# A two-layer hybrid encoder: residual rows, post-norm gains and memory operands issued at single steps of the output projection, and three memory steps ahead of layer two

## The chip, the cores and the metric

The kernel runs on one core of a Trainium2 chip. The metric is the device time of one execution in microseconds (us). Engines are named as in the profile: PE (TensorE, matmul), PEld (its weight loads), DVE (VectorE), ACT (ScalarE), POOL (GpSimd) and SP (SyncE). POOL and SP do hardly more here than issue DMAs; queue q0 is POOL's, queue q1 is SP's.

## What is computed

Two layers, each with the same parts. Sequence 512, width 2048, 256 memory tokens, all in float32:

```python
for l in range(2):
    h = rmsnorm(x, pre_norm_g[l])
    z = h @ w_in[l]                       # splits: latents, conv parts, memory query, gate
    a_out = mla_attention(...)            # from the latents
    c_out = short_gated_conv(...)
    mem_n = rmsnorm(mem, mem_norm_g[l])
    m_out = memory_attention(q_mem, mem_n, w_mk[l], w_mv[l])   # mk = mem_n @ w_mk, mv = mem_n @ w_mv
    y = concat([a_out, c_out, m_out]) * silu(gate)
    o = y @ w_o[l]                        # 2048 x 2048: the output projection
    x = x + rmsnorm(o, post_norm_g[l])    # post-norm and residual
```

## The kernel before

**Number format.** Each float32 operand is split into a high part (`wh`, a rounding cast on ACT, L179) and a low part (`wl`, the difference, on DVE, L180). One product is three matmuls: high by high, high by low, low by high (L252 to L254). A weight must have been loaded (`wr`), cast and subtracted before its matmuls can start; the first of a step needs `wh`, the second `wl`.

**The products.** A projection multiplies blocks of two by two in seven products, P1 to P7, instead of eight. The output projection runs in two pairs of output columns, `g0` and `g1`, 2 x 512 columns each. Each is a list of passes: P2, P1, P5, P6, then P3 and P7 alternating, then P4. A pass has four steps, c = 0 to 3, one for each 256 rows of a quarter of the weights; a step is twelve matmuls. P3/P7 has eight steps. The P2 passes of both pairs run earlier, inside the attention. What is left of a pair, `g0[1:]` or `g1[1:]`, is P1 (steps 1 to 4), P5 (5 to 8), P6 (9 to 12), P3/P7 (13 to 20), P4 (21 to 24).

**Weights.** Sums of weight blocks are formed in two ways. P1 loads a block into a tile T; P5 adds a second block on DVE (L170); P6 and P4 add a third and a fourth by an *accumulating load* (`more`, L135 with `accum_op`), which POOL issues into the same `wr` tile as soon as the last reader of its older contents is done. P7 adds a block to P3's on DVE (L170). All other loads are plain ones that SP issues (512 KB each). There are eight `wr` tiles; four of them hold T all through a pair, so P3 and P7 have four. There are three `wh` and three `wl` tiles. In layer two's second pair the split of P4's weights goes into slabs of its own, `T4h` and `T4l`.

**Around it.** `fetch(t)` loads row block t of the residual (`xr`, 1 MB) on POOL; `gains(g)` loads the two post-norm gain blocks of a pair (`g2`, 256 KB each) on POOL. When a row block has its four column blocks, `residual` sums the squares, adds the row block to the residual (L1162), writes it to `xs`, and in layer one normalises it (L543, L549) for layer two. `mem_reload` reads the transposed, split memory (`mH`, `mL`, two of each, 1 MB apiece) back from DRAM on POOL. Layer two begins with sixteen memory steps (`mk`, `mv`), between which the normalised rows are transposed (`hps`, L562), sixteen groups of four; step t waits for row block t.

**Order.** PE, SP and POOL execute in the order in which the program is written, with weights prepared two steps ahead. The order on DVE and ACT is set by a scheduler from dependences and its own estimates, so it can change where the text of those engines does not.

Of the kernel before, what the change touches and what calls it, by code (L numbers as in the profile page):

```python
# [6 lines left out]
F32R = mybir.dt.float32r  # L7
# [9 lines left out]
NT = S // P  # L17
# [61 lines left out]
class Program:  # L79
# [19 lines left out]
    def add(self, fn, units=(), room=0.0, ahead=None):  # L99

        self.steps.append((list(units), fn, room, self.ahead if ahead is None else ahead))
# [106 lines left out]
def encoder(tc, x, mem, positions, pre_norm_g, w_in, q_norm_g, w_uq, kv_norm_g, w_ukv, conv_w,  # L208
# [3 lines left out]
    nc = tc.nc  # L212
    depth = w_in.shape[0]
# [15 lines left out]
    add = pr.add  # L229

    G = {}
    n_id = [0]

    def nm(s):
        n_id[0] += 1
        return f"{s}_{n_id[0]}"
# [4 lines left out]
    def slab(name, dt=F32):  # L241
        return slabs.tile([P, D], dt, tag="slab", name=nm(name))
# [310 lines left out]
    def transpose_rows(l, t, src, quarters=range(4), on=None):  # L553

        if quarters[0] == 0:
            G[f"hT{t}"] = slab("hT").rearrange("p (k c) -> p k c", c=P)
        hT = G[f"hT{t}"]
        g = G[f"g1_{l}"].rearrange("p (k o) -> p k o", o=1)
        for q in quarters:
            ps = bank("hps")  # L560
            for j in range(4):
                nc.tensor.transpose(ps[:, j * P:(j + 1) * P], src[:, (4 * q + j) * P:(4 * q + j + 1) * P], G["ident"])  # L562
            if (on or (nc.vector if t < 2 else nc.scalar)) is nc.vector:
                nc.vector.tensor_tensor(hT[:, 4 * q:4 * q + 4, :], ps.rearrange("p (j c) -> p j c", j=4),
                                        g[:, 4 * q:4 * q + 4, :].broadcast_to([P, 4, P]), op=ALU.mult)
            else:
                for j in range(4):
                    nc.scalar.activation(hT[:, 4 * q + j, :], ps[:, j * P:(j + 1) * P], AF.Copy,
                                         scale=g[:, 4 * q + j, :])

    def left_half(tt, halves=(0, 1)):
        hT = G[f"hT{tt}"]
        for h in halves:
            G["left"].split(("A11", "A12")[h], tt, hT[:, 8 * h:8 * h + 8, :])
# [11 lines left out]
    def first_factor(t):  # L586
        G[f"hs{t}"] = slab("hs")
        G[f"r{t}"] = row_factor(G[f"x{t}"], G[f"hs{t}"])

    def first_rows(t, halves=(0, 1)):  # L590
        for h in halves:
            c = slice(h * 1024, (h + 1) * 1024)
            nc.vector.tensor_scalar_mul(G[f"hs{t}"][:, c], G[f"x{t}"][:, c], G[f"r{t}"])
# [78 lines left out]
            for i in range(2):  # L672
                nc.gpsimd.dma_start(G["mTd"][2 * (q // 4) + i], G["mT"][-1][i].bitcast(F32))

    def mem_reload(h):
        two = slab("mH", F32R), slab("mL", F32R)
        for i in range(2):
            nc.gpsimd.dma_start(two[i], G["mTd"][2 * h + i])
        G.setdefault("mT", []).append(two)

    def mem_kt(kt, sl=slice(None)):
        return tuple(t.rearrange("p (k c) -> p k c", c=256)[:, kt % 8, sl] for t in G["mT"][kt // 8])
# [506 lines left out]
    def put(*passes):  # L1189
        for steps in passes:  # L1190
            for s in steps:
                add(*s)
# [26 lines left out]
    for l in range(depth):  # L1219
        G["left"] = L = Left(True)  # L1220
        C, gs, owns = projection(l)

        def use(L=L):
            G["left"] = L
            G["ys"] = {}
        turn = [lambda l=l, t=t: transpose_rows(l, t, G[f"hs{t}"]) for t in range(NT)]
        if l == 0:
            add(use)
            def turn_half(t, h, on=None):
                return lambda: transpose_rows(0, t, G[f"hs{t}"], (2 * h, 2 * h + 1), on)  # L1230
            add(turn_half(0, 0))
            add(lambda: first_rows(1, (0,)))
            add(pr.begin_prep(1))
            add(lambda: left_half(0, (0,)))
            add(pr.begin_prep(2))
            add(turn_half(1, 0, nc.scalar))
            add(lambda: first_rows(1, (1,)))
            add(lambda: left_half(1, (0,)))
            add(pr.begin_prep(3))
            add(lambda: first_factor(2))  # L1240
            add(turn_half(0, 1))
        else:
            ms = mem_steps(l)
            put(ms[:1])
            add(use)
            for n in range(16):
                t, q = n // 4, n % 4
                if q == 0:
                    add(lambda t=t: pr.until(lambda: f"hs{t}" in G))
                add(lambda t=t, q=q: transpose_rows(l, t, G[f"hs{t}"], (q,)))  # L1250
                if t < 2 and q % 2:
                    add(lambda t=t, q=q: left_half(t, (q // 2,)))
                if t >= 2 and q == 3:
                    add(lambda t=t: right_half(t - 2))
                put(ms[n + 1:n + 2])
        (a, b), (a1, b1) = gs[0][:2], gs[1][:2]
        add(owns[0])
        if l == 0:
            put(a[:1])
            add(first.close)  # L1260
            add(turn_half(1, 1))
            add(lambda: left_half(0, (1,)))
            add(lambda: left_half(1, (1,)))
            add(lambda: first_rows(2))
            add(lambda: first_factor(3))
            add(lambda: first_rows(3))
            put(a[1:], b[:1])
            add(turn[2])
            add(lambda: right_half(0))
            put(b[1:3])  # L1270
            add(turn[3])
            add(lambda: right_half(1))
            put(b[3:])
        else:
            put(a, b)
        add(owns[1])
        put(a1, b1)
        put(*gs[0][2:], *gs[1][2:])
        add(owns[2])
        put(gs[2][0])  # L1280
        conv = [(conv_turn(l, c, C), []) for c in range(4)]
        put(weave(gs[2][1] + gs[2][2], conv, 2), *gs[2][3:])
        add(owns[3])
        put(*gs[3])
        add(owns[4])
        add(lambda l=l: latents_rows(l))
        if l == 0:
            add(positions_load)
        g4 = [s for steps in gs[4] for s in steps]
        put(g4[:4])  # L1290
        add(lambda l=l, C=C: latents_begin(l, C))
        put(g4[4:8])
        if l > 0:
            add(lambda C=C: k_rope(C))
        put(g4[8:16])
        if l == 0:
            add(mem_load)
            G["mTd"] = dram.tile([4, P, D], F32, name="mTd")
        lat = [latent_turn("cq", j) for j in range(4)] + [latent_turn("ckv", j) for j in range(2)] + [k_rope_turn] * (l > 0)
        gm = lambda t, C=C: C["gm"][:, t, :]  # L1300
        more = [(f, []) for f in lat + [qm_turn(j, C) for j in range(4)] + [gate_turn(12 + j, gm, j) for j in range(4)]]
        if l == 0:
            more.insert(8, (mem_rows, []))
        put(weave(g4[16:], more[:11], 1))
        put(more[11:])
        gates = [gate_turn(j, lambda t, C=C, j=j: C["ga0" if j < 4 else "ga1"][:, t, :], j % 4) for j in range(8)]
        G["left"] = Y = Left(False)
        g0, g1, gains, fetch = out_proj(l)

        def low(p):  # L1310
            return lambda: G["left"].split("A12", p, G["ys"][2 + p][:, :, :256])

        def use_y(Y=Y):
            G["left"] = Y

        def sums(p):
            def f():
                a, b = G["ys"][p], G["ys"][2 + p]
                left = G["left"]
                pr.defer(1.2, lambda: left.split("A11", p, a[:, :, :256]))  # L1320
                pr.defer(1.2, lambda: left.split("A22", p, b[:, :, 256:]))
                combine(left, p, a[:, :, :256], b[:, :, :256], a[:, :, 256:], b[:, :, 256:])
            return f

        last_pair = {0: [(sums(0), []), g0[0][0]], 1: [g0[0][1]], 2: [g0[0][2]], 3: [g0[0][3]],
                     4: [g1[0][0]], 5: [g1[0][1]], 6: [g1[0][2]], 7: [g1[0][3]]}
        mixer(l, C, gates, {6: [(use_y, []), (low(0), [])], 7: [(low(1), [])]}, last_pair)
        add(sums(1))
        add(gains(0))
        put(*g0[1:])  # L1330

        def route(l=l):
            if l == depth - 1:
                G["src"], G["dst"] = G["dst"], out[0]
            else:
                G["src"], G["dst"] = x[0], dram.tile([S, D], F32, name="xs")
        add(route)
        add(gains(1))
        put(*g1[1:3])
        put(g1[3])  # L1340
        for t in range(NT):
            add(fetch(t))
        if l + 1 < depth:
            add(lambda: mem_reload(0))
        put(g1[4])
        if l + 1 < depth:
            add(lambda: mem_reload(1))
        put(g1[5])
        if l + 1 == depth:
            add(pr.settle)  # L1350

# [26 lines left out]
```

## Time and profile before

| | |
|---|---|
| runs | 1545.78, 1545.6, 1544.92 us; median 1545.6 |
| profiled execution | span 1547.0 us, which is its time; mean granted PE clock 0.989 |
| busy: PE, PEld, DVE, ACT, POOL | 1502.5, 1285.7, 1165.6, 864.6, 179.8 us |
| layer one: g0's P3/P7, P4 | 677 to 699, to 710 us |
| layer one: g1's P6, P3/P7, P4 | 732 to 743, to 772, to 783 us |
| layer two: its output projection | the same 752.2 us later, up to g1's P3/P7 |

The profile is of one execution. A timeline row gives the start, the duration, the engine, the line and operation, output and inputs, and in brackets the idle time before it and what ended it. Where one product's matmuls follow one another without a gap, they start 0.23 us apart, and a step of twelve takes 2.73 us.

### The profile page before, as it was taken

The page shows a single profiled execution, that of the slowest core. Times are in us where ns is not written, and L with a number is a line of the kernel's source. Part 1 is how long each engine was busy: PE and PEld are TensorE (multiplying, and loading weights), DVE is VectorE, ACT ScalarE, POOL GpSimd, SP SyncE. Part 2 cuts the span into 40 slices and gives each one's busy share as a digit, 9 for nine tenths or more (in the row PEclk, how much of TensorE's full clock was granted, in tenths as well). Part 3 has the DMA queues.
Part 4 walks back from the last instruction along what each step waited for, and adds up shares of the span by engine and source line. Part 5 has one row for each costly group of instructions (what it writes and reads, how often), then busy time and mean ns, then how long its engine had stood idle before and what let it go on. Part 6 is the DMA issues. An engine that isn't in the chain of part 4 may idle for free.

```text
span 1547.0 us, 20323 instructions
## 1 busy us (share of the span) xinstructions
PE 1502.5 (97%) x7613; PEld 1285.7 (83%) x7613; DVE 1165.6 (75%) x1510; ACT 864.6 (56%) x1335; POOL 179.8 (12%) x201
## 2 busy tenths in 40 slices
PE   9999999999999999999899999999999999999996
PEld 7778888987898888888688888888988888888874
DVE  6977887576777768887597977787686586789866
ACT  7543434454657768645379533534454586775542
POOL 1112020221000000021120112020211000002030
PEclk9999999999999999999999999999999999999998
DMA  8789695979473202397987889685978511037693
GB/s 327 190 199 238 179 192 159 202 197 235 150 243 98 68 29 69 105 212 183 325 304 241 235 216 236 179 189 158 206 201 201 164 55 42 28 112 157 196 269 137
DMA packets 146934, 275.59 MB, mean 178 GB/s; under 512 B 17340, under 2 KB 40212, under 8 KB 143508
## 3 DMA queue, kind: packets, MB, share of 16 engines
q1 hardware_dynamic: 111568, 189.84, 39.1%
q0 software_dynamic: 35136, 84.42, 26.3%
q8 instruction: 59, 0.97, 0.3%
q14 instruction: 39, 0.32, 0.1%
q10 hardware_dynamic: 132, 0.05, 0.0%
HBM read 259.59 MB, written 14.68 MB: 177 GB/s over the span
## 4 chain that ended last, share of the span: by engine, by line
PE 83%; DVE 5%; DMA 4%; ACT 4%; issue 3%; POOL 1%; DVEq 0%; POOLq 0%; ACTq 0%
PE P L253 19%; PE P L254 19%; PE P L252 19%; DMA wr<-in_w_o_dram 2%; PE ptp L980 2%; DMA wr<-in_w_in_dram 2%; DVE wl L180 2%; PE tps L738 1%; PE o L253 1%; PE sc L252 1%; PE sc L253 1%; ACT wh L179 1%; PE sc L254 1%; PE o L254 1%; PE o L252 1%
## 5 line engine op out<-in xcount | busy, mean ns | idle before, releaser
L179 ACT CAST wh<-wr 128x1024 fp32r<-128x1024 f32 (+1 forms) x408 | 420.4, 1032 | 501.5 <-PE P L254 278.6
L180 DVE TENSOR_TENSOR wl<-wr,wh 128x1024 fp32r<-128x1024 f32 (+1 forms) x408 | 485.8, 1195 | 232.9 <-ACT wh L179 231.8
L252 PE MATMUL P<-wh,S 128*128 128x512 f32 (+1 forms) x896 | 349.8, 390 | 8.5 <-ACT wh L179 6.0
L253 PE MATMUL P<-wl,S 128*128 128x512 f32 (+1 forms) x896 | 348.3, 389 | 7.8 <-DVE wl L180 7.8
L254 PE MATMUL P<-wh,S 128*128 128x512 f32 (+1 forms) x896 | 347.0, 387 | 0.7 <-DVE S L258 0.7
L252 PE MATMUL P<-wh,A 128*128 128x512 f32 (+1 forms) x656 | 253.8, 387 | 0.2 <-ACT wh L179 0.2
L253 PE MATMUL P<-wl,A 128*128 128x512 f32 (+1 forms) x656 | 252.3, 385 | 1.3 <-DVE wl L180 1.3
L254 PE MATMUL P<-wh,A 128*128 128x512 f32 (+1 forms) x656 | 252.4, 385 | 0.5 <-DVE A L258 0.5
L253 PEld LDWEIGHTS P<-wl,S 128*128 128x128 f32 x896 | 170.5, 190 | 40.4 <-DVE wl L180 10.7
L252 PEld LDWEIGHTS P<-wh,S 128*128 128x128 f32 x896 | 170.0, 190 | 40.7 <-ACT wh L179 7.7
L254 PEld LDWEIGHTS P<-wh,S 128*128 128x128 f32 x896 | 170.3, 190 | 32.4 <-DVE S L258 1.2
L135 POOL DMA_DIRECT2D wr<-in_w_in_dram x80 | 96.9, 1212 | 565.2 <-DVE wl L180 431.5
L170 DVE TENSOR_TENSOR wr<-wr,wr 128x1024 f32<-128x1024 f32 (+1 forms) x112 | 133.5, 1194 | 14.0 <-DMA wr<-in_w_o_dram 6.1
L253 PEld LDWEIGHTS P<-wl,A 128*128 128x128 f32 x656 | 123.7, 189 | 23.4 <-DVE wl L180 1.7
L254 PEld LDWEIGHTS P<-wh,A 128*128 128x128 f32 x656 | 123.4, 188 | 23.6 <-DVE A L258 1.2
L252 PEld LDWEIGHTS P<-wh,A 128*128 128x128 f32 x656 | 123.7, 189 | 22.5 <-ACT wh L179 0.7
L966 ACT ACTIVATE P<-sc,nm 128x512 f32<-128x512 f32 (+1 forms) x96 | 60.0, 624 | 36.4 <-DVE nm L963 35.8
L969 ACT ACTIVATE P<-P,rec 128x512 f32<-128x512 f32 (+1 forms) x96 | 62.1, 658 | 5.1 <-DVE rec L968 5.1
L963 DVE TENSOR_REDUCE nm<-sc 128x1 f32<-128x512 f32 (+1 forms) x96 | 57.2, 596 | 10.0 <-PE sc L961 6.3
L258 DVE TENSOR_TENSOR PT<-ptp,PT 128x512 fp32r<-128x512 f32 (+1 forms) x96 | 56.5, 594 | 8.2 <-ACT PT L257 7.8
L135 POOL DMA_DIRECT2D wr<-in_w_o_dram x32 | 38.6, 1206 | 157.8 <-DVE wl L180 141.7
L185 DVE SCALAR_TENSOR_TENSOR wl<-wr,cols,wh 128x512 fp32r<-128x512 f32 x64 | 45.8, 746 | 14.2 <-ACT wh L184 14.0
(268 smaller groups left out, 2221.1 us busy)
## 6 DMA issues: line engine op xcount, KB each, us to landing
wr<-in_w_in_dram SPq DMA_DIRECT2D x176, 512.0 KB, 4.4
wr<-in_w_o_dram SPq DMA_DIRECT2D x80, 512.0 KB, 4.0
wr<-in_w_in_dram POOLq DMA_DIRECT2D x64, 512.0 KB, 7.3
wr<-in_w_in_dram SPq DMA_DIRECT2D x40, 416.0 KB, 3.8
wr<-in_w_o_dram POOLq DMA_DIRECT2D x32, 512.0 KB, 7.2
wr<-in_w_mk_dram SPq DMA_DIRECT2D x16, 512.0 KB, 4.5
wr<-in_w_mv_dram SPq DMA_DIRECT2D x16, 512.0 KB, 4.2
wr<-in_w_in_dram POOLq DMA_DIRECT2D x16, 416.0 KB, 5.7
```

The costliest lines, as they stand in the source:

```text
L135: engine.dma_start(dst, src, **kw)
L170: nc.vector.tensor_tensor(src, src, tiles[c], op=ALU.add)
L179: nc.scalar.copy(hi[:, :n], src)
L180: nc.vector.tensor_tensor(lo[:, :n], src, hi[:, :n].bitcast(F32), op=ALU.subtract)
L185: nc.vector.scalar_tensor_tensor(lo[:, h], src[:, h], g, hi[:, h].bitcast(F32), op0=ALU.mult, op1=ALU.subtract)
L252: nc.tensor.matmul(ps, ah, bh, start=first, stop=False, **kw)
L253: nc.tensor.matmul(ps, ah, bl, start=False, stop=False, **kw)
L254: nc.tensor.matmul(ps, al, bh, start=False, stop=last, **kw)
L258: nc.vector.tensor_tensor(lo, src, hi.bitcast(F32), op=ALU.subtract)
L963: nc.vector.tensor_reduce(nmax, ps, axis=AX.X, op=ALU.max, negate=True)
L966: nc.scalar.activation(pt, ps, AF.Exp, bias=nmax, accum_out=tot)
L969: nc.scalar.activation(pt, pt, AF.Copy, scale=rec)
```

## The change

Before, the gains of the second pair are written behind the whole first pair; the four residual rows and half of the memory stand behind P6 and P3/P7 of the second pair, and the other half behind the next pass. After, a helper `among` writes each of them behind a numbered step. Layer two begins with three memory steps in place of one, and each later one is two transposes earlier in the list. `mem_reload` takes one tile instead of two.

```diff
-    def mem_reload(h):
-        two = slab("mH", F32R), slab("mL", F32R)
-        for i in range(2):
-            nc.gpsimd.dma_start(two[i], G["mTd"][2 * h + i])
-        G.setdefault("mT", []).append(two)
+    def mem_reload(i):
+        t = slab(("mH", "mL")[i % 2], F32R)
+        nc.gpsimd.dma_start(t, G["mTd"][i])
+        if i % 2 == 0:
+            G["mT half"] = t
+        else:
+            G.setdefault("mT", []).append((G.pop("mT half"), t))
...
-            put(ms[:1])
+            put(ms[:3])
...
-                put(ms[n + 1:n + 2])
+                put(ms[n + 3:n + 4])
...
         add(gains(0))
-        put(*g0[1:])
...
-        add(gains(1))
-        put(*g1[1:3])
-        put(g1[3])
-        for t in range(NT):
-            add(fetch(t))
+        def among(passes, at):
+            for n, s in enumerate([s for steps in passes for s in steps], 1):
+                add(*s)
+                if n in at:
+                    add(at[n])
+
+        among(g0[1:], {14: fetch(0), 17: fetch(1), 20: fetch(2), 22: gains(1)})
+        at = {5: fetch(3)}
         if l + 1 < depth:
-            add(lambda: mem_reload(0))
-        put(g1[4])
-        if l + 1 < depth:
-            add(lambda: mem_reload(1))
-        put(g1[5])
+            at.update({n: lambda i=i: mem_reload(i) for i, n in enumerate((8, 10, 13, 16))})
+        among(g1[1:], at)
```

Line numbers behind `mem_reload` are three higher afterwards (L1132, L1162 and L1096 become L1135, L1165 and L1099).

POOL, layer one's output projection, before, from the first pair's last accumulating loads (wr142 to wr145) to the memory's first half; wr158 to wr161 are the second pair's T tiles, filled for P6 and then for P4:

```order
L135 DMA wr144_5564<-in_w_o_dram 128x2x512
L135 DMA wr145_5619<-in_w_o_dram 128x2x512
L1096 DMA g2_629_6409<-in_post_norm_g_dram 128x512
L1096 DMA g2_630_6411<-in_post_norm_g_dram 128x512
L135 DMA wr158_6243<-in_w_o_dram 128x2x512
L135 DMA wr159_6261<-in_w_o_dram 128x2x512
```

```order
L135 DMA wr160_6280<-in_w_o_dram 128x2x512
L135 DMA wr161_6304<-in_w_o_dram 128x2x512
L1132 DMA xr_635_6648<-in_x_dram 128x2048
L1132 DMA xr_636_6650<-in_x_dram 128x2048
L1132 DMA xr_637_6652<-in_x_dram 128x2048
L1132 DMA xr_638_6654<-in_x_dram 128x2048
L678 DMA mH_639_6656<-mTd_81 128x2048
L678 DMA mL_640_6657<-mTd_81 128x2048
```

The same places after, first the end of the first pair, then the second pair's accumulating loads:

```order
L135 DMA wr145_5619<-in_w_o_dram 128x2x512
L1135 DMA xr_629_6211<-in_x_dram 128x2048
L1135 DMA xr_630_6264<-in_x_dram 128x2048
L1135 DMA xr_631_6333<-in_x_dram 128x2048
L1099 DMA g2_632_6373<-in_post_norm_g_dram 128x512
L1099 DMA g2_633_6375<-in_post_norm_g_dram 128x512
```

```order
L135 DMA wr160_6285<-in_w_o_dram 128x2x512
L1135 DMA xr_638_6517<-in_x_dram 128x2048
L135 DMA wr161_6309<-in_w_o_dram 128x2x512
L135 DMA wr158_6246<-in_w_o_dram 128x2x512
L135 DMA wr159_6266<-in_w_o_dram 128x2x512
L678 DMA mH_639_6579<-mTd_81 128x2048
L135 DMA wr160_6285<-in_w_o_dram 128x2x512
L135 DMA wr161_6309<-in_w_o_dram 128x2x512
L678 DMA mL_640_6619<-mTd_81 128x2048
L678 DMA mH_643_6678<-mTd_81 128x2048
L678 DMA mL_646_6732<-mTd_81 128x2048
```

Three rows moved directly behind the first pair's last accumulating load, ahead of the gains; row 3 and the first memory operand stand between the second pair's accumulating loads, and three memory operands behind the last of them. Layer two's output projection has the same order without the memory.

ACT, layer two's second pair, before and after. wh430 and wh431 are P6's c=2 and c=3, wh432 and wh433 P3's and P7's c=0, and so on; the four T4h are P4's held weights, which need its accumulating loads:

```order
L179 CAST wh430_13158<-wr334_12866 128x1024
L179 CAST wh431_13177<-wr335_12890 128x1024
L179 CAST wh432_13196<-wr340_13074 128x1024
L179 CAST wh433_13215<-wr340_13074 128x1024
L179 CAST wh434_13241<-wr342_13116 128x1024
L179 CAST wh435_13260<-wr342_13116 128x1024
L179 CAST T4h_1266_13332<-wr332_12829 128x1024
L179 CAST wh436_13278<-wr344_13156 128x1024
L179 CAST T4h_1266_13332<-wr333_12847 128x1024
L179 CAST T4h_1268_13350<-wr334_12866 128x1024
L179 CAST T4h_1268_13350<-wr335_12890 128x1024
```

```order
L179 CAST wh430_13166<-wr334_12870 128x1024
L179 CAST T4h_1266_13332<-wr332_12831 128x1024
L179 CAST wh431_13185<-wr335_12894 128x1024
L179 CAST T4h_1266_13332<-wr333_12851 128x1024
L179 CAST wh432_13204<-wr340_13080 128x1024
L179 CAST T4h_1268_13350<-wr334_12870 128x1024
L179 CAST T4h_1268_13350<-wr335_12894 128x1024
L179 CAST wh433_13223<-wr340_13080 128x1024
L179 CAST wh434_13241<-wr342_13124 128x1024
```

The four T4h moved ahead of wh431, wh432 and wh433; DVE's T4l moved with them.

DVE at the start of layer two, before and after. wl222, wl223, wl224 are the weights of the first three memory steps; `xr<-og,r,xr` is the residual sum of row block 1; L1122 (L1125) multiplies by a gain, L437 adds P1:

```order
L185 SCALAR_TENSOR_TENSOR wl222_6879<-wr174_6730,cols_197,wh222_6878 128x512 x2
L1122 TENSOR_TENSOR og_569_5633<-og_569_5633,g2_630_6411 128x512
L1122 TENSOR_TENSOR og_573_5644<-og_573_5644,g2_630_6411 128x512
L185 SCALAR_TENSOR_TENSOR wl223_6910<-wr175_6748,cols_197,wh223_6909 128x512 x2
L437 TENSOR_TENSOR og_569_5633<-og_569_5633,P1_631_6417 128x512
L1162 SCALAR_TENSOR_TENSOR xr_636_6650<-og_571_5642,r_655_6874,xr_636_6650 128x1024 x2
L437 TENSOR_TENSOR og_573_5644<-og_573_5644,P1_632_6418 128x512
L185 SCALAR_TENSOR_TENSOR wl224_6932<-wr176_6767,cols_197,wh224_6931 128x512 x2
```

```order
L185 SCALAR_TENSOR_TENSOR wl222_6879<-wr174_6734,cols_197,wh222_6878 128x512 x2
L1125 TENSOR_TENSOR og_569_5633<-og_569_5633,g2_633_6375 128x512
L1125 TENSOR_TENSOR og_573_5644<-og_573_5644,g2_633_6375 128x512
L1165 SCALAR_TENSOR_TENSOR xr_630_6264<-og_571_5642,r_655_6874,xr_630_6264 128x1024 x2
L185 SCALAR_TENSOR_TENSOR wl223_6910<-wr175_6752,cols_197,wh223_6909 128x512 x2
L437 TENSOR_TENSOR og_569_5633<-og_569_5633,P1_634_6423 128x512
L437 TENSOR_TENSOR og_573_5644<-og_573_5644,P1_635_6424 128x512
L185 SCALAR_TENSOR_TENSOR wl224_6932<-wr176_6771,cols_197,wh224_6931 128x512 x2
```

The residual sum of row block 1 moved ahead of wl223. On ACT the two halves of wh223 and of wh224 each moved to both sides of a normalisation (L543 or L549).

## The prediction

> **What bounds the kernel now.** I read the page first: the shares of the engines and the chain of work that ended last.
>
> ```profile
> span 1547.0 us, 20323 instructions
> PE 1502.5 (97%) x7613; PEld 1285.7 (83%) x7613; DVE 1165.6 (75%) x1510; ACT 864.6 (56%) x1335; POOL 179.8 (12%) x201
> PE 83%; DVE 5%; DMA 4%; ACT 4%; issue 3%; POOL 1%; DVEq 0%; POOLq 0%; ACTq 0%
> ```
>
> TensorE bounds nearly everything, so this change, which adds no arithmetic, can only open or close holes in TensorE's work. Next I asked for stretches (start:end and length, then busy time of PE, PEld, DVE, ACT and POOL, then the granted clock, the DMA share and GB/s) around the places that the diff touches, all in layer one's output projection and the start of layer two.
>
> ```profile
> 677.00:710.00 33.00, 33.00 (x147) 27.34 (x146) 26.21 (x28) 16.47 (x23) 0.00 (x0) 1.00 0.68 222
> 750.00:760.00 10.00, 6.00 (x26) 4.26 (x24) 2.49 (x3) 2.10 (x2) 0.00 (x0) 1.00 1.04 412
> 760.00:770.00 10.00, 8.59 (x28) 6.18 (x29) 5.61 (x5) 3.99 (x4) 0.00 (x0) 0.83 0.84 299
> 810.00:820.00 10.00, 7.70 (x41) 6.47 (x40) 7.98 (x10) 9.66 (x16) 2.71 (x7) 0.83 0.69 232
> ```
>
> The first pair's P3/P7 (677 to 699) has no hole at all. The second pair's P3/P7 has one around 760, while the DMA engines are full. The third sits in layer two's first steps. TensorE's own timeline names what ended each wait:
>
> ```profile
> 687.66 0.39 PE L253 MATMUL P<-wl,S 128*128 128x512 f32 x1
> 690.38 0.39 PE L253 MATMUL P<-wl,S 128*128 128x512 f32 x1
> ...
> 753.91 0.50 PE L253 MATMUL P<-wl,S 128*128 128x512 f32 x1 [0.77 <-DVE wl L180]
> 759.98 0.49 PE L252 MATMUL P<-wh,S 128*128 128x512 f32 x1 [3.24 <-ACT wh L179]
> 761.24 0.80 PE L253 MATMUL P<-wl,S 128*128 128x512 f32 x1 [0.77 <-DVE wl L180]
> 761.84 0.63 PE L254 MATMUL P<-wh,S 128*128 128x512 f32 x1
> 764.39 0.39 PE L254 MATMUL P<-wh,S 128*128 128x512 f32 x1
> ...
> 814.18 0.66 PE L562 MATMUL hps<-identr,og 128*128 128x128 f32 x4 [2.31 <-ACT og L549]
> ```
>
> The hole of the second pair is 3.24 + 0.77 + 0.77, and a 0.64 later: 5.4 us. Six matmuls issued from 761.84 to 764.39 are 0.43 us apart where 687.66 to 690.38 holds twelve, 0.23 apart; with the stretched one at 761.24 a hole costs about 1.6 us of slow matmuls behind it. Counted against twelve matmuls of 0.23 a step, the pair loses 7.7. [...]
>
> What is late at 759.98 is a load. POOL's and SP's own timelines, and the DMA issues of single windows (the last number is us from issue to landing), show why:
>
> ```profile
> 672.48 1.19 POOL L135 DMA_DIRECT2D wr<-in_w_o_dram  x1 [2.20 <-DVE wl L180]
> 673.20 1.62 POOL L1096 DMA_DIRECT2D g<-in_post_norm_g_dram  x2
> ...
> 737.45 1.20 POOL L135 DMA_DIRECT2D wr<-in_w_o_dram  x1 [1.26 <-DVE wl L180]
> 738.17 2.65 POOL L1132 DMA_DIRECT2D xr<-in_x_dram  x4
> ```
> ```profile
> 674.91 8.27 SPq L135 DMA_DIRECT2D wr<-in_w_o_dram  x4
> 740.19 8.27 SPq L135 DMA_DIRECT2D wr<-in_w_o_dram  x4
> ```
> ```profile
> wr<-in_w_o_dram POOLq DMA_DIRECT2D x1, 512.0 KB, 7.4
> ...
> wr<-in_w_o_dram SPq DMA_DIRECT2D x1, 512.0 KB, 11.2
> ...
> wr<-in_w_o_dram SPq DMA_DIRECT2D x1, 512.0 KB, 14.8
> ```
> ```profile
> wr<-in_w_o_dram POOLq DMA_DIRECT2D x1, 512.0 KB, 6.2
> ...
> wr<-in_w_o_dram SPq DMA_DIRECT2D x1, 512.0 KB, 7.1
> ```
>
> These five are: the last accumulating load of the second pair (issued 737.45, landed 744.85); SP's loads of 740.19 and 742.61, which landed 11.2 and 14.8 later, at 751.4 and 757.4; then for the first pair its last accumulating load (672.48, landed 678.7) and SP's second load (677.33, landed 684.4). So behind the last accumulating load, call it E, SP's two loads of the second pair landed at E + 6.55 and E + 12.55, 6.0 us each, while four residual rows and half the memory (6 MB) moved on POOL's queue:
>
> ```profile
> DMA packets 2897, 10.22 MB, mean 365 GB/s; under 512 B 218, under 2 KB 218, under 8 KB 2128
> q0 software_dynamic: 1002, 6.54, 59.5%
> q1 hardware_dynamic: 1894, 3.66, 37.0%
> ...
> xr<-in_x_dram POOLq DMA_DIRECT2D x1, 1024.0 KB, 17.7
> ```
>
> q0 is POOL's queue, q1 SP's (742:770). The fourth row, issued near 740.4, landed near 758, 13 us after E: 3.2 us a megabyte.
>
> **The change, part by part.** The order on POOL decides. POOL does not wait for TensorE's steps; it runs ahead until an accumulating load waits for a split. "One by one between the steps" is thus not how they will be issued.
>
> (1) First pair, both layers: +10.6. Rows 0 to 2 and two gains now stand behind the last accumulating load with nothing between them, as the gains alone did at 673.20. They issue in one burst, 673.2 to about 676 (four took 2.65 at 738.17): 3.5 MB instead of 0.5, in front of SP's loads of 674.91 and 677.33, which feed steps P3 and P7 of c=2. In the second pair the way from landing to the lo matmul was 753.91 − 751.4 = 2.5 for a P3 load and 761.24 − 757.4 = 3.84 for a P7 load. In the first pair these matmuls stand at 687.66 and 690.38, so the loads must land by 685.2 and 686.5. With E = 678.7 the first lands at E + 6.55 = 685.3: in time by a hair. The second at E + 12.55 = 691.2 if the burst lasted; 3.5 MB at 3.2 us each end at E + 11.2, so its last part is quick: about 690.3. That is 3.8 late, plus 1.6 of slow matmuls, less a little that the hi matmul takes up: 5.3. Layer two's first pair has the same order and shifted times: 5.3 again. Bounds: 0 as in the trace of before (7.1 from issue to landing), 7.0 with 691.2 and a worse clock, for each.
>
> (2) Second pair, layer one: +1.5. The memory's last three megabytes still stand behind the last accumulating load, and row 3 and the first memory operand now stand between accumulating loads, on a queue that is full there:
>
> ```profile
> DMA packets 2159, 4.19 MB, mean 190 GB/s; under 512 B 120, under 2 KB 120, under 8 KB 2158
> ...
> q0 software_dynamic: 1614, 3.13, 77.9%
> ```
>
> (716:738, mostly 200 GB/s: accumulating loads go at half the rate of plain ones.) Each megabyte there costs 2.6 us at 400 GB/s, so E moves from 744.85 to about 750.1. SP's loads, 2 us later, land near 756.7 and 759.7; the first, P3's, is now 6 late, the second 2.3 later than before. Loss 9.2 against 7.7. Bounds: −7.7 (hole gone) and +4.
>
> (3) Start of layer two: +1.3. Three memory steps instead of one ahead of the transposes give the normalised rows two steps (2.8 us each) more; the 2.31 wait and its slow matmuls, together 4.1, go. But VectorE's and ScalarE's order changes there:
>
> ```profile
> 783.50 0.91 POOL L264 TENSOR_TENSOR r<-ms,mhalf 128x1 f32<-128x1 f32 x1
> ...
> 784.51 2.47 DVE L1162 SCALAR_TENSOR_TENSOR xr<-og,r,xr 128x1024 f32<-128x1024 f32 x2
> ...
> 785.69 0.60 PE L562 MATMUL hps<-identr,og 128*128 128x128 f32 x4
> 786.05 0.47 PE L252 MATMUL mv<-wh,mH 128*128 128x512 f32 x1
> ```
>
> The second memory step's operand wl223 now stands behind the 2.47 of residual row 1, which waits for POOL to 784.4; wl223 comes at about 786.9 (two parts, 0.7 each, from there) while TensorE, without the transpose between, wants it at 785.69: 1.5 to 1.9 late. The third step's wh224 has a half on each side of a 2.01 us normalisation on ScalarE: later again, 4.3 in all by my hand schedule, and 1.1 more at P1's c=2. 5.4 − 4.1 = 1.3; bounds −4.1 and +3.
>
> (4) Second pair, layer two: +1.8. No memory is loaded there; the 4 MB of rows shrink to one. But the held splits of P4 (T4h, T4l) now stand ahead of weights that are needed earlier:
>
> ```profile
> 1498.95 1.05 ACT L179 CAST T4h<-wr 128x1024 fp32r<-128x1024 f32 x1
> 1504.92 1.04 ACT L179 CAST wh<-wr 128x1024 fp32r<-128x1024 f32 x1 [4.92 <-DMA wr<-in_w_o_dram]
> 1505.87 2.94 ACT L179 CAST T4h<-wr 128x1024 fp32r<-128x1024 f32 x3
> ...
> 1489.64 1.22 POOL L135 DMA_DIRECT2D wr<-in_w_o_dram  x1 [1.29 <-DVE wl L180]
> ```
>
> Now wh431 (P6, c=3) waits for T4h c=0, whose load is 2.6 later for row 3: lo near 1495.9, 3.4 late. Only then is P4's last load issued (1489.64 before, 1496.3 now), landing 6.2 to 7.4 later, and wh433 (P7, c=0) stands behind its split: about 1506 instead of 1498. Loss 10.3 with slow matmuls; the hole of before (waits of 0.91, 0.76, 1.83 and 1.76, and slow matmuls) was 8.5. Bounds −5 and +4.
>
> Nothing is added to SP, and POOL issues one instruction for one as before. Moving gains(1) and row 0 earlier gains nothing, since the first use is after 698. Sum: 10.6 + 1.5 + 1.3 + 1.8 = +15.2, on the span 1547.0 of the profiled execution: 1562.2. That execution stands 1.4 above the median 1545.6, so 1560.8.
>
> **Rivals.**
> - Faster: the bursts are small enough. If SP's second load in the first pair lands by 686.5, 9.2 us after issue, term 1 is nothing, and if the second pair's first load still lands by 751, its 7.7 go. The 7.1 of before speaks for it, the 11.2 and 14.8 against. −7.7 + 1.3 + 1.8 = −4.6: 1541. It decides at these two landings. Chance 0.09.
> - First pair covered, the rest as above: 1545.6 + 4.6 = 1550.2. What separates it from the forecast is how the queues share. The ratio above is by packets: q0's are 6.5 KB on the mean, q1's 1.9. [...] Chance 0.12.
> - Layer two's start covers its late operands: term 3 is −4.1, 1555.4. For it: wl223's wait is short. Chance 0.14.
> - Deeper holes: both first pairs lose the 7.7 that the second pair lost, as when all four megabytes arrive at once: 1565.6. Chance 0.2.
> - No change: the slow places trade evenly, within 3 us (0.2%, about what a measurement can tell) of 1545.6. Only if term 1 halves and term 2 wins back the rest. Chance 0.07.
>
> **How the numbers follow.** The forecast itself holds 0.38. Slower: 0.38 + 0.12 + 0.14 + 0.2 = 0.84; same 0.07; faster 0.09. Range 1549 (first pairs covered) to 1568 (deeper holes, with 2 for term 4's bound); the faster and unchanged cases, 0.16, lie outside it.
>
> **What would show it.** Right: at 687 to 692 a wait of TensorE of 2 to 4 us ended by ACT wh or DVE wl, with a clock below 1 there, again 752 us later; SP's load of 677.33 landing 12 to 14 us after issue; no wait before the last transposes of layer two, but one before its second memory step; ACT idle before T4h in layer two's second pair for a DMA, with P7's c=0 late by some 8. Wrong: no hole at 690, or the hole at 760 gone. The sum falls if POOL issues the rows apart, or if the loads share evenly.

## The result, and the profile after

The changed kernel takes 1562.66 us (median of 4 runs, 1559.39 to 1565.94) against 1545.69 (4 runs): a ratio of 1.011, 95% interval 1.0096 to 1.0123. The profiled execution has a span of 1564.1 us. The forecast was 1560.8.

First, where it went. The table holds the lengths of the stretches between the same matmuls in both timelines (start times subtracted), and what the prediction gave for them.

| stretch | before | after | difference | predicted |
|---|---|---|---|---|
| start to the first pair's P5 | 654.79 | 653.43 | −1.36 | 0 |
| layer one, first pair, P5 to P7 | 43.53 | 51.07 | +7.54 | +5.3 |
| layer one, second pair, P5 to P7 | 51.86 | 50.76 | −1.10 | +1.5 |
| second pair's P4 to layer two's P5 | 110.61 | 112.22 | +1.61 | +1.3 |
| layer two, to the first pair's P5 | 524.48 | 525.22 | +0.74 | 0 |
| layer two, first pair, P5 to P7 | 43.52 | 50.98 | +7.46 | +5.3 |
| layer two, second pair, P5 to P7 | 52.74 | 54.98 | +2.24 | +1.8 |
| the rest (P4 and P1 twice, the end) | 65.47 | 65.44 | −0.03 | 0 |

The sum is +17.1. Two of the differences, −1.36 and +0.74, stand where the change touches nothing: the stretch ahead of the first pair's P5 took 649.4 to 654.8 in the thirteen profiles of this document, though the program is the same there. Without holes, P5 to P7 is 43.5. From TensorE's timeline of the changed kernel, most of the rows with a wait, and the first and last of a slow stretch:

```profile
687.67 0.50 PE L253 MATMUL P<-wl,S 128*128 128x512 f32 x1 [0.76 <-DVE wl L180]
...
692.65 0.80 PE L252 MATMUL P<-wh,S 128*128 128x512 f32 x1 [2.19 <-ACT wh L179]
...
693.91 0.80 PE L253 MATMUL P<-wl,S 128*128 128x512 f32 x1 [0.46 <-DVE wl L180]
694.50 0.63 PE L254 MATMUL P<-wh,S 128*128 128x512 f32 x1
...
698.77 0.63 PE L252 MATMUL P<-wh,S 128*128 128x512 f32 x1
...
759.97 0.50 PE L253 MATMUL P<-wl,S 128*128 128x512 f32 x1 [0.32 <-DVE wl L180]
...
766.07 0.50 PE L252 MATMUL P<-wh,S 128*128 128x512 f32 x1 [3.30 <-ACT wh L179]
...
791.80 0.50 PE L253 MATMUL mv<-wl,mH 128*128 128x512 f32 x1 [0.64 <-DVE wl L185]
...
796.74 0.39 PE L252 MATMUL mk<-mH,wh 128*128 128x256 f32 x1 [1.78 <-ACT wh L184]
...
1453.35 0.53 PE L252 MATMUL P<-wh,S 128*128 128x512 f32 x1 [2.35 <-ACT wh L179]
...
1507.70 0.49 PE L252 MATMUL P<-wh,S 128*128 128x512 f32 x1 [1.31 <-ACT wh L179]
...
1509.15 0.50 PE L253 MATMUL P<-wl,S 128*128 128x512 f32 x1 [0.96 <-DVE wl L180]
...
1519.95 0.80 PE L252 MATMUL P<-wh,S 128*128 128x512 f32 x1 [5.27 <-ACT wh L179]
```

Each place that the prediction named has its wait, and the wait of 2.31 for the rows (814.18 before) is gone. POOL's timeline of the changed kernel, and in windows at 673.55, 675.97 and 671.12 the landing times of SP's two loads and of the last accumulating load:

```profile
671.12 1.20 POOL L135 DMA_DIRECT2D wr<-in_w_o_dram  x1 [2.20 <-DVE wl L180]
671.84 2.15 POOL L1135 DMA_DIRECT2D xr<-in_x_dram  x3
673.47 1.59 POOL L1099 DMA_DIRECT2D g<-in_post_norm_g_dram  x2
```
```profile
wr<-in_w_o_dram SPq DMA_DIRECT2D x1, 512.0 KB, 11.6
...
wr<-in_w_o_dram SPq DMA_DIRECT2D x1, 512.0 KB, 14.2
...
wr<-in_w_o_dram POOLq DMA_DIRECT2D x1, 512.0 KB, 6.0
```

Three rows and the gains go out in one burst of 3 us. SP's second load takes 14.2 instead of 7.1.

### The profile page after: what moved, and what is told of

Read it like the earlier page. It is cut to its first block, busy times and chain, and to the rows that moved or that the text cites. A ratio compares the mean times of both kernels' runs of the same rounds, so it can differ in the third digit from the quotient of the medians.

```text
span 1564.1 us, 20318 instructions
## 1 busy us (share of the span) xinstructions
PE 1510.3 (97%) x7613; PEld 1288.9 (82%) x7613; DVE 1164.8 (74%) x1510; ACT 863.9 (55%) x1335; POOL 179.3 (11%) x201
## 4 chain that ended last, share of the span: by engine, by line
PE 33%; issue 6%; DVE 4%; DMA 4%; ACT 2%; POOL 1%; POOLq 0%; DVEq 0%; ACTq 0%
PE P L253 7%; PE P L254 7%; PE P L252 7%; DMA wr<-in_w_o_dram 2%; DMA wr<-in_w_in_dram 1%; DVE wl L180 1%; PE ptp L983 1%; PE tps L741 1%; DVE wr L170 1%; ACT wh L179 1%; PE o L253 1%; PE sc L252 1%; PE sc L253 1%; DVE xr L1165 1%; PE sc L254 1%
## 5 line engine op out<-in xcount | busy, mean ns | idle before, releaser
L252 PEld LDWEIGHTS P<-wh,S 128*128 128x128 f32 x896 | 171.5, 191 | 50.4 <-ACT wh L179 17.1
L184 ACT ACTIVATE wh<-wr,cols 128x512 fp32r<-128x512 f32 x64 | 43.8, 718 | 22.6 <-PE mk L253 8.0
```

What stands on the lines that cost most here:

```text
L184: nc.scalar.activation(hi[:, h], src[:, h], AF.Copy, scale=g)
L252: nc.tensor.matmul(ps, ah, bh, start=first, stop=False, **kw)
```

## The experiments

Each was timed beside the kernel before; "ratio" is to it (its medians there were 1545.7 to 1546.5). "Less than the changed kernel" is the difference from 1562.66. Runs of one kernel spread over some 6 us, up to 9, so profiles are compared by stretch: "the pair" is P5 to P7 of an output pair, "the end" is what follows layer two's second pair.

**One part alone: three memory steps.**

```diff
-            put(ms[:1])
+            put(ms[:3])
...
-                put(ms[n + 1:n + 2])
+                put(ms[n + 3:n + 4])
```

> The kernel before with one part of the change alone: three memory steps ahead of layer two's transposes. Theory A (the late operands at layer two's start come from the earlier residual rows, which let the scheduler put row 1's sum ahead of the second step's operand; the three steps alone are a gain): VectorE's order keeps that operand ahead of row 1, no wait before the second or third memory step, the wait of 2.31 and its slow matmuls gone: 4.1 less, about 1541.6 us. Theory B (with three steps the second and third operand are late whatever the order): the waits of 0.64, 1.78 and 0.28 are there too, 1546 to 1547 us.

Measured 1545.34, ratio 0.9993 (0.9981 to 1.0005): no difference. Row 1's sum stands behind wl223 here, and the waits of 0.64, 1.78 and 0.28 are indeed absent, but others come, on a memory step's low part later on:

```profile
814.86 0.38 PE L254 MATMUL mk<-mH,wl 128*128 128x256 f32 x1 [1.64 <-DVE wl L185]
822.10 0.38 PE L254 MATMUL mk<-mH,wl 128*128 128x256 f32 x1 [0.48 <-DVE wl L185]
...
841.70 0.50 PE L253 MATMUL P<-wl,A 128*128 128x512 f32 x1 [0.32 <-DVE wl L180]
```

The stretch from P4 to layer two's P5 is 109.77, 0.84 less than before, not 4.1. Theory A is right that wl223 stays ahead and wrong on the gain; B is wrong on the waits.

**One part alone: the first pair.** In the kernel before, `among(g0[1:], {14: fetch(0), 17: fetch(1), 20: fetch(2), 22: gains(1)})`; row 3 and half of the memory stay behind P6 of the second pair, the other half behind P3/P7.

> The kernel before with the first pair's part alone: rows 0 to 2 and the gains written into the first pair, row 3 and the memory where they were, one memory step. Theory A (the burst behind the first pair's last accumulating load delays SP's loads; the burst in the second pair shrinks by the same 3 MB and its hole a little): first pair 7.5 longer in each layer, second pair of layer one 2.5 shorter, layer two's second pair about 4.5 shorter though the held splits stand ahead of P7's first weights, layer two's start unchanged: +8, about 1553.7 us. Theory B (the first pair's holes come from the change as a whole, not from the rows written there): no hole near 687 to 692 and the smaller burst shows as a gain, below 1543 us.

Measured 1544.94, ratio 0.9992 (0.9982 to 1.0003). The first pairs are 49.68 and 49.87, 6.2 and 6.4 longer, with waits at the same steps as in the changed kernel: theory B falls. But the second pairs fall to 46.13 and 47.80, 5.7 and 4.9 shorter, where I had 2.5 and 4.5: three megabytes fewer in the second pair are worth nearly what three in the first cost. The rest came from layer two's start, unchanged in order, 1.7 shorter: its wait is 1.68 instead of 2.31 and no slow matmuls follow it.

**Rows in SP's own queue.**

```diff
-                nc.gpsimd.dma_start(st["x"][t], G["src"][t * P:(t + 1) * P, :])
+                (nc.sync if t < 3 else nc.gpsimd).dma_start(st["x"][t], G["src"][t * P:(t + 1) * P, :])
```

> The changed kernel with rows 0 to 2 issued by SP instead of POOL, written at the same steps; SP's queue then has them behind the loads of P3/P7 and ahead of the second pair's first loads. Theory A (two queues share the DMA engines, and the rows overtake SP's loads): with the rows in SP's own queue the first pair's holes go in both layers, 7.5 each, and the second pair's P1 loads have the slack: 15 less than the changed kernel, about 1547.7 us. Theory B (3 MB more at this place cost the same on any queue): about 1562 us, holes of 7 or waits before the second pair's P1 instead.

Measured 1549.65, ratio 1.0019 (1.001 to 1.0028): 13 less than the changed kernel. Both first pairs are 43.52, without a wait (start:end, length, busy PE, PEld, DVE, ACT, POOL, clock, DMA share, GB/s), at a DMA share of 0.94:

```profile
673.00:696.00 23.00, 23.00 (x103) 19.06 (x102) 17.22 (x17) 10.17 (x13) 0.00 (x0) 1.00 0.94 311
```

That is theory A's outcome. But SP issues the rows at 680.14, 684.68 and 691.92, between its own loads, so this run changes the queue and the spacing at once and can't tell which of the two did it.

**Rows really spread.** The changed kernel, with a gate ahead of each moved load, row 3 and the memory included (the line that keeps the newest low part as `pr.lo` is not shown):

```diff
...
+        def gate(f):
+            def g():
+                nc.gpsimd.tensor_scalar(small(1, "gate"), pr.lo[:, :1].bitcast(F32), 1.0, 0.0, op0=ALU.mult, op1=ALU.add)
+                f()
+            return g
...
-        among(g0[1:], {14: fetch(0), 17: fetch(1), 20: fetch(2), 22: gains(1)})
+        among(g0[1:], {14: gate(fetch(0)), 17: gate(fetch(1)), 20: gate(fetch(2)), 22: gate(gains(1))})
-        at = {5: fetch(3)}
+        at = {5: gate(fetch(3))}
...
-            at.update({n: lambda i=i: mem_reload(i) for i, n in enumerate((8, 10, 13, 16))})
+            at.update({n: gate(lambda i=i: mem_reload(i)) for i, n in enumerate((8, 10, 13, 16))})
```

> The changed kernel with a gate ahead of each moved load on POOL: a 1-element POOL operation that reads the newest low part (wl) prepared at the step where the load is written, so that the load can't be issued before that step. Theory A (the change does not spread the loads, POOL issues rows 0 to 2 as one burst, and the burst is what costs): rows 0 to 2 are issued near 681, 688 and 697 and delay SP's loads by at most one megabyte; first pair's loss 0 to 0.5 instead of 7.5 in each layer; second pair of layer one 3 less, that of layer two as in the changed kernel, since its held splits stand where they stood: 18 less, about 1544.5 us. Theory B (3 MB among SP's loads cost the same, spread or not): about 1562 us.

Measured 1549.25, ratio 1.0015 (1.0006 to 1.0024). POOL's timeline:

```profile
677.77 0.61 POOL L1136 DMA_DIRECT2D xr<-in_x_dram  x1
684.76 1.21 POOL L1344 TENSOR_SCALAR gate<-wl 128x1 f32<-128x1 f32 x1 [6.38 <-DVE wl L180]
685.91 0.60 POOL L1136 DMA_DIRECT2D xr<-in_x_dram  x1
```

The first pairs are 43.52 and 44.38: the same 3 MB, on the same queue, at the same places in the program, cost 0 and 0.9 when they are apart, instead of 7.5. Theory B falls. The second pairs disappoint, 49.75 (1 less than the changed kernel, not 3) and 57.53 (2.5 more); row 3 and the memory are gated there too, and why it costs more in layer two isn't settled.

**One row instead of three in the first pair.**

```diff
-        among(g0[1:], {14: fetch(0), 17: fetch(1), 20: fetch(2), 22: gains(1)})
+        among(g0[1:], {14: fetch(0), 22: gains(1)})
...
-        add(fetch(3))
+        for t in range(1, NT):
+            add(fetch(t))
```

(made from the run with the first pair alone)

> The kernel before with one row (0) and the gains in the first pair, three rows left in the second. Theory A (a threshold: SP's second load must land by its deadline; 1.5 MB in the burst let it land in time): no hole in the first pair, second pair of layer one about as before, layer two's up to 1.5 less: 1543 to 1546 us. Theory B (loss in proportion to the burst): 2.5 in each first pair, about 1550 us.

Measured 1540.59, ratio 0.9964 (0.9954 to 0.9975): faster than both kernels. SP's second load takes 9.4, and TensorE waits once in the first pair:

```profile
wr<-in_w_o_dram SPq DMA_DIRECT2D x1, 512.0 KB, 9.4
...
688.05 0.50 PE L253 MATMUL P<-wl,S 128*128 128x512 f32 x1 [0.66 <-DVE wl L180]
```

With 7.1 for 0.5 MB, 9.4 for 1.5 MB and 14.2 for 3.5 MB behind the last accumulating load, a megabyte costs SP's second load 2.3 to 2.4 us, but TensorE pays only beyond the 9.2 that the prediction worked out as the deadline: 1.06 and 0.91 here. That is nearer to the threshold of theory A (it had no hole) than to B's 2.5. Layer two's second pair is 48.13, 4.6 shorter where A had at most 1.5, so the whole is below A's range.

**The held splits.** Three runs of the changed kernel; the first takes the held tiles away:

```diff
-        g1 = group(G["left"], ("o", l, 1), 512, block(1), slot(1), SECOND, fin(1), hold if last else None)
+        g1 = group(G["left"], ("o", l, 1), 512, block(1), slot(1), SECOND, fin(1), None)
```

> The changed kernel without the held splits: P4's weights in layer two's second pair are split into the ordinary tiles, in the written order, so nothing stands ahead of wh431 to wh433. Theory A (term 4 of the prediction: the scheduler's new order costs): layer two's second pair falls from 55.0 to 46 or 47 from P5 to P7, about 8 less than the changed kernel: 1554.5 us. Theory B (row 3 among the accumulating loads costs, not the order): it stays above 52, about 1561 us.

Measured 1551.66, ratio 1.0033 (1.0021 to 1.0045), 11 less than the changed kernel. Layer two's second pair is 43.52, 11.5 shorter, with row 3 where it was: theory B falls. The end is 24.56 instead of 21.93: without the held tiles the program can't finish P4 row by row. To leave them in and change the order alone, VectorE and ScalarE were put into written order all through that pair:

> The changed kernel with one thing undone: VectorE's and ScalarE's instructions of layer two's second pair stand in written order, the held splits behind P7's last weights. Theory A (the scheduler's order is the cause of the second pair's 55.0): P5 to P7 there falls to 43.5 to 45, end stays 22.0: 10 to 11.5 less than the changed kernel, 1551 to 1552.5 us. Theory B (row 3 among the accumulating loads is part of it): P5 to P7 stays above 48, 1556 us or more.

Measured 1563.19, ratio 1.0117 (1.0104 to 1.013), in theory B's range, though it doesn't show B's cause: the pair falls to 48.41, and of its waits those at P5 (1.03, 0.75 and 0.52) are new, while 0.38 and 0.75 are left at P6; the end grows to 31.44. The same written order in the version at the end of this section ("the run before" in the text on record):

> The kernel of the run before (rows in the first pair's P4, memory in the second pair's P3/P7) with the held splits back, and VectorE's and ScalarE's instructions of layer two's second pair in written order, which has T4h and T4l behind P7's last weights. Theory A (held splits shorten the end by the 2.6 that their absence cost, 24.55 against 21.95, and in this order they delay nothing): P5 to P7 still 43.5 to 43.7, end 22.0: 2.5 less, about 1526.4 us. Theory B (written order loses at the additions and copies of the results what it wins): 1529 us or more.

Measured 1540.88, ratio 0.9966 (0.9955 to 0.9978): pair 46.74, end 31.41: theory B. So written order throughout costs the end 9.5. Confined to the steps that matter, in the last layer alone (the condition and the line that makes `late` are not shown):

```diff
...
+            at.update({11: lambda: late.enter_context(tc.manual_schedule(
+                engines={mybir.EngineType.DVE, mybir.EngineType.Activation})), 19: late.close})
```

> The changed kernel with one thing undone: from step 11 to step 19 of layer two's second pair VectorE's and ScalarE's order is written order, which puts T4h and T4l behind P7's last weights. Theory A (the scheduler's order is what makes the second pair 55.0 long): P5 to P7 there 43.5 to 46, end 22.0: 9 to 11.5 less than the changed kernel, 1551 to 1553.5 us. Theory B (row 3 among the accumulating loads makes it): P5 to P7 above 50, 1557.5 us or more.

Measured 1552.52, ratio 1.004 (1.0025 to 1.0055). The pair is 43.55, no wait at all, with row 3 where it was among the accumulating loads: theory A for the pair. The end is 24.11, not 22.0, so 2.2 of the 11.4 is paid there. TensorE is busy in 44 of 44:

```profile
1486.00:1530.00 44.00, 44.00 (x196) 36.39 (x195) 29.58 (x28) 20.54 (x24) 9.04 (x8) 1.00 0.77 181
```

**A version made from this.** Rows gated into the first pair's P4, memory into the second pair's P3/P7, no held tiles, three memory steps (the gate and the line without held tiles as above):

```diff
+        among(g0[1:], {20: gate(fetch(0)), 21: gate(fetch(1)), 22: gate(fetch(2)), 23: gate(fetch(3)), 24: gains(1)})
+        at = {}
         if l + 1 < depth:
+            at.update({n: gate(lambda i=i: mem_reload(i)) for i, n in enumerate((17, 18, 19, 20))})
+        among(g1[1:], at)
```

> Built from the findings: all four rows gated into the first pair's P4 (steps 20 to 23), the four memory operands gated into the second pair's late P3/P7 (steps 17 to 20), P4's weights in layer two's second pair split like layer one's (no T4h, T4l), three memory steps. Theory A (all holes of both pairs come from rows and memory in SP's way, or from the held splits): P5 to P7 takes 43.5 in all four pairs, 8.3 and 9.2 less than before in the second ones; layer two's start 0.8 less as with three steps alone: 18 less than before, about 1528 us. Theory B (SP's loads are late for the accumulating loads alone, without rows or memory): second pairs still lose 3 or more each, 1534 us or above.

Measured 1528.88 (1527.64 to 1532.81), ratio 0.9885 (0.9872 to 0.9898), as theory A has it. The pairs are 43.52, 44.18, 43.52 and 43.61: the accumulating loads alone don't make SP's loads late, and theory B falls. Layer one's second pair has TensorE full and the clock at 1.00 where both kernels had their hole:

```profile
740.00:764.00 24.00, 24.00 (x108) 19.88 (x107) 18.53 (x19) 11.27 (x14) 2.46 (x4) 1.00 0.93 269
```

With held tiles and the order confined as above:

> Rows in the first pair's P4 and memory in the second pair's P3/P7, held splits kept; VectorE's and ScalarE's order is written order only from step 11 (P6) to step 19 (P3/P7) of layer two's second pair, so that T4h and T4l stand behind P7's last weights and the rest is the scheduler's as before. Theory A (the losses of the fully written order were at P5 and at the end, outside these steps): P5 to P7 43.6, end 22.0: about 1526.3 us. Theory B (the end needs the early splits): end 24.5 or more, 1529 us or above.

Measured 1531.51, ratio 0.9901 (0.9886 to 0.9917): no gain over the run before; the pair is 43.74 and the end 23.72, between the theories, the time in B's range.

## Why the prediction was right, point by point

**Term 1 (+10.6; measured +15.0) was right in mechanism and short in size.** The burst, the two loads, the two late steps and both layers came as written, and the gated run shows that the burst and not the rows as such costs (0 and 0.9 there against 7.5). Two sizes were off. SP's first load, "in time by a hair", came 1.3 late (waits of 0.17 and 0.76), but the second was later still and set the loss. SP's second load landed 14.2 after issue, 690.17; the forecast of 690.3 stood in the times of before, 1.36 later, so the load was 1.2 later than expected. And the slow matmuls behind the hole lasted from 692.65 to 699.2 and not 3 us: some 3 us lost instead of 1.6. The step that fell short is "plus 1.6 of slow matmuls". It was read from one hole, and it is one of two values: in the ten first pairs with this burst (five kernels) the slow matmuls cost 1.6 to 1.7 six times and 2.6 to 3.0 four times, and this profile had the dearer value in both layers. What went with each is in the last section. So +15.0 is the upper end: the same two first pairs lost 12.1 to 14.5 in the profiles of the other four kernels.

**Term 2 (+1.5; measured −1.1) had the wrong mechanism.** I let SP's first load wait for E, the last accumulating load. The windows at 748.12, 750.53 (SP) and 746.12 (POOL's last accumulating load) of the changed kernel show:

```profile
wr<-in_w_o_dram SPq DMA_DIRECT2D x1, 512.0 KB, 9.4
...
wr<-in_w_o_dram SPq DMA_DIRECT2D x1, 512.0 KB, 13.0
...
wr<-in_w_o_dram POOLq DMA_DIRECT2D x1, 512.0 KB, 11.9
```

SP's first load landed at 757.5, before E at 758.0, and not 6.6 behind it; the second at 763.5, as late against its step as before. E did move, from 744.85 to 758.0: 6.2 of that is the shift of the whole stretch, 7.0 is its own; I had 5.2. The step "the first is now 6 late" failed: its low part makes TensorE wait 0.32 at 759.97, where it waited 0.77 before. This, and the 0.64 of before at 769.31, which is gone, makes the 1.1. Why the first load is served earlier here isn't settled.

**Term 3 (+1.3; measured +1.6)** had the right places: 0.64 (forecast 1.5 to 1.9) at the second memory step, 1.78 and 0.28 at the third, and a slow stretch behind them. The run with three steps alone keeps wl223 ahead, and so does the run with the first pair alone, which has rows 0 to 2 early; only the whole change moves it. So neither part gives that order by itself, and which combination does isn't shown. The credit of −4.1 for the three steps can't be had alone either: there the 2.31 and its slow matmuls went, but the waits of 1.64, 0.48 and 0.32 came in their place, and 0.84 was left. The slow matmuls that the credit counted don't follow every such wait: in the kernel before, 3.41 us at half clock (from 815.58) came behind the 2.31, in the run with the first pair alone none came after the 1.68.

**Term 4 (+1.8; measured +2.2)** came as written. ScalarE's timeline of the changed kernel:

```profile
1505.65 1.05 ACT L179 CAST T4h<-wr 128x1024 fp32r<-128x1024 f32 x1 [5.85 <-DMA wr<-in_w_o_dram]
1506.60 1.04 ACT L179 CAST wh<-wr 128x1024 fp32r<-128x1024 f32 x1
...
1517.90 1.04 ACT L179 CAST T4h<-wr 128x1024 fp32r<-128x1024 f32 x1 [6.07 <-DMA wr<-in_w_o_dram]
1518.86 1.99 ACT L179 CAST wh<-wr 128x1024 fp32r<-128x1024 f32 x2
```

ScalarE stands 5.85 and 6.07 in front of T4h, with the weights of P6's c=3 and P7's c=0 behind it. With written order from P6 to P3/P7 the pair lost nothing (43.55); as far as P7's last weights, ScalarE's order then differs from the changed kernel's in T4h alone, and VectorE's in T4l and one more exchange of two neighbours. So the order makes the whole loss, and row 3 no part of it. Both halves of the term are borne out: the hole of before, 9.2 (8.5 in the forecast), is emptied by the change, and the new order puts one of 11.4 (10.3) in its place.

The sum hit, 15.2 against 17.1 in the profiles, and part of that is luck: terms 1 and 2 erred in opposite directions, by 4.4 and 2.6. Of the rivals, "deeper holes" (1565.6) was nearest; its condition, 7.7 lost in both first pairs, nearly came (7.54 and 7.46), and the miss of term 2 took part of that back.

## What to carry to other kernels

A load written between two steps goes out there only if its queue's engine has something to wait for there. POOL, with only DMAs to issue, ran ahead to its next dependence: rows and gains written behind steps 14, 17, 20 and 22 all left between 671.84 and 675.06, as a burst; with a gate ahead of each, the rows left at 677.77, 685.91 and 693.41. Look for the transfers that other queues have in flight behind that point, and work out their deadlines: with SP's second load at 7.1 us from issue to landing TensorE lost nothing here, with 9.4, just beyond the deadline of 9.2, it lost 1.06, with 14.2 it lost 7.54. After any move, read the order of the scheduled engines too: an instruction that waits for a late transfer and stands ahead of one needed sooner can cost all that the move won (11.4 here, where 9.2 had been emptied).

## What the runs showed of the hardware

Slow matmuls behind a wait came in stretches of about 3 us or about 6, and not behind every wait. The 3.3 us wait of layer one's second pair was followed by one stretch of the short kind in each profile with it; one of 2.19 (692.65) by 6.5; waits of 1.33 and 0.76, 0.62 and 0.77 in layer two with one row by none. The same code lost 5.8 to 7.7 in the first pairs of five kernels. In the traces the slow stretches are those at a lower granted clock. From 100 us on, until TensorE has long idle times at the end, it fell to 0.5 for 3.41 or 6.83 us and nothing else, and the falls of one profile are whole multiples of 3.41 us apart (760.96 and 815.58 before: 16 of them). The windows around the first pair's hole in the changed kernel, and two of the run with one row around its wait of 2.14 at 810.70 (start:end, length, busy PE, PEld, DVE, ACT, POOL, clock, DMA share, GB/s):

```profile
685.68:689.10 3.42, 2.49 (x10) 1.54 (x9) 1.22 (x1) 0.68 (x1) 0.00 (x0) 1.00 0.99 325
689.10:692.51 3.41, 1.36 (x6) 0.77 (x5) 1.23 (x1) 0.96 (x2) 0.00 (x0) 1.00 0.62 236
692.51:695.92 3.41, 2.81 (x6) 1.93 (x7) 3.26 (x3) 1.03 (x2) 0.00 (x0) 0.50 0.69 199
695.92:699.34 3.42, 3.42 (x10) 2.68 (x9) 1.55 (x2) 1.33 (x2) 0.00 (x0) 0.50 0.73 232
699.34:702.75 3.41, 3.41 (x17) 2.81 (x16) 2.52 (x3) 1.49 (x2) 0.00 (x0) 1.00 0.55 189
...
806.65:810.06 3.41, 1.91 (x16) 1.71 (x15) 2.09 (x4) 3.07 (x4) 1.49 (x4) 1.00 0.72 222
810.06:813.48 3.42, 2.78 (x14) 2.38 (x15) 3.42 (x4) 3.42 (x8) 1.09 (x2) 1.00 0.61 241
```

With the span divided into windows of 3.41 us, counted from a fall, the falls went with TensorE's idle time within one window, not with the length of a wait. In the profiles of the two kernels, from 100 to 1513 us, windows at full clock with 2.02 us of idle or more were followed by half clock in 9 of 9 cases, one with 1.67 was too, and of six with 0.9 to 1.6 none was. Counted over all thirteen profiles, it was 43 of 43 with 1.93 or more, none of 41 with 0.9 to 1.6, and 8 of 13 between these. Of the thirteen windows at half clock in the two kernels' profiles, the three that still had 0.60, 0.73 and 0.85 of idle were followed by a second; the ten with 0.55 or less were not. In the changed kernel half clock came behind the waits of 2.19 (from 692.51) and 1.78 (from 798.32). The wait of 2.14 fell across two windows, which had 1.50 and 0.64 of idle, and cost nothing beyond itself. Where the windows lay differed from profile to profile of the same code: ahead of the first pair, where the two programs are the same, half clock came from 344.54 and from 385.50 before, 3.41 us each, and from 381.90 after, 6.83 us. The 1.6 and the 3 of term 1 are one window and two.

What the prediction says of the two queues has these numbers in the profile of before. From 745 to 757, with POOL's rows and SP's loads in flight, each queue moved 545 packets, 3.95 MB on q0 and 1.05 MB on q1. From 716 to 738, with accumulating loads on POOL's queue, q0 moved 3.13 MB in 77.9% of the DMA engines' time, which makes 183 GB/s; the rows, plain loads, moved their 3.95 MB in 79.2% of 745 to 757, which makes 416 GB/s.
